# Side work of an MLP's Strassen pairs handed out at other points of the pair, and one row of means that stays in SBUF

## The chip, the cores and the metric

The kernel runs on one core of a Trainium2 chip. The metric is the device time of one execution, in microseconds (us). The kernel before takes 1814.26 us (median of 3 runs, 1813.84 to 1816.24). The five engines named below are PE (TensorE, matmul), DVE (VectorE), ACT (ScalarE), POOL (GpSimd) and SP (SyncE, which issues all DMAs here).

## The reference

The program is one layer of an encoder on 1536 tokens of width 1024: an input projection, attention and pooling heads, an output projection, then a squared-ReLU MLP and a gated per-layer embedding. The change lies in the MLP, of which the reference computes, per token,

```python
h = x + heads @ w_out
n = rmsnorm(h, g_mlp)                       # mean of squares over 1024, eps 1e-6
h = h + square(relu(n @ w_up)) @ w_down     # w_up 1024x4096, w_down 4096x1024
```

All of it is float32.

## The kernel before

**Tokens and hidden units.** The MLP works on 3 chunks `c` of 512 tokens and, in each, on 16 pairs `g` of 256 hidden units, so 48 pairs in a row, here numbered 0 to 47 (pairs 16 and 32 begin a chunk). A tile of 128x1024 floats fills one of 49 slots of SBUF, and a new tile waits until the last user of its slot is done. A float32 product is made of three fp32r matmuls, high by high, high by low, low by high (`three`), so every operand exists as a rounded high part and a low part (the rest).

**One pair.** The up projection of a pair is done by a scheme of seven half-size products instead of eight, in the order 1, 6, 2, 5, 7, 3, 4 (`Pair.run`). Each is 12 matmuls 128x256 in one of four PSUM banks: products 1 and 2 in `px`, 6 in `py`, 5 and 3 in `pz`, 7 and 4 in `pq`. Products 2, 3 and 4 add to what is in their bank, so they may start only when the bank has been read: product 3 waits for `u4` (DVE, L866), product 4 for the sum into `c2` (DVE, L870). ACT copies product 1 to `t`, DVE makes `u2`, `u4` and the four sums of `c1` and `c2`, ACT applies the ReLU and the squares, and DVE takes the low parts of the squares `r` (L886).

**The down projection** of a pair runs one pair later, in four blocks (`down`, blocks d0 to d3), each of 12 matmuls 128x512 and an evacuation on DVE that adds it to `h` (L837). They stand between the products of the next pair: product 1, d0, 6, 2, d1, 5, 7, d2, 3, 4, d3. The last product of a pair is thus followed by d3 of the pair before it, by product 1 of the next pair, and then by its own d0, which is the first to read its `r`. Inside a block the loop over the output half `e` is outside that over the hidden half `f`. With the order of `three`, the second matmul of d0 is the first that reads the low part of `r[0]`, the fifth the first that reads that of `r[1]`.

**Side work.** `after(i)` is called right behind the evacuation of each product and hands out one step each of: `feeding`, which prepares the next pair's weights (`feed`: a cast on ACT, the low part on POOL, and four sums `s1` to `s4` on DVE, L793 to L804; at its step 3 it loads the raw weights `wur` of the pair after that); `splits`, high and low parts of this pair's `w_down` (`split_down`: cast on ACT, low part on POOL for the first half, on DVE for the second, L816 and L817); in a chunk's first pair `raising` (`raise_h`, L662, multiplies `h` by the row `ws[c]` of mean squares, on DVE, eight steps); and `step()`, the next step of a list of chores: in pairs 1 to 11 or so of a chunk the squares of the next chunk (`make_m`), and the scaling, squares and gate inputs of the last one (`finishing`, with multiplications on DVE, L1138 and L1128). In the last pair of a chunk it also loads the next chunk's operands (`load_mo`). The `after` behind product 4 comes ahead of the two low parts of `r`.

**What sets the order.** PE, ACT, DVE and POOL run in the order in which the program is written, SP in an order made by a scheduler. DMAs use eight semaphores in turn, so an issue waits for the transfer eight before it.

**Mean squares of a chunk.** `make_m` ends with a row of means, brought to all partitions by a matmul, in `acc[:, 1]`; it is stored to `w_d[c]` in DRAM (L647) and loaded into `ws[c]` by `load_ms` at the chunk's first pair. `invert` later writes the reciprocals to the same `w_d[c]`. For chunk 0 this falls at the start of the MLP, where also `h` of chunk 0 comes back from DRAM (`load_h`), `h` of chunk 2 is stored there (`spill`), and `wur` of pair 1 is loaded, when `feeding` reaches its step 3.

Of the kernel before, what the change touches and what calls it, by code (L numbers as in the profile page):

```python
# [12 lines left out]
ALU = mybir.AluOpType  # L13
# [22 lines left out]
def encoder_layer(ctx, tc, xT, xn, xr, pT, w1, w2, w_pool, w_out, w_up, w_down, w_gate, w_proj,  # L36
# [23 lines left out]
    def as32(ap):  # L60
        return ap.bitcast(F32)
# [533 lines left out]
    def make_m(c, et, el):  # L595

        A, B = slice(0, HF), slice(HF, CH)
        acc = slot([P, 2, CH], F32, f"sqm{c}")  # L600

        def squares_of(b, m):
            for i in range(2):
                sq = slot([P, 2, CH], F32, f"sqm{c}{b}{i}")
                for h in range(2):
                    out = sq[:, h] if b + i + h else acc[:, 0]
                    yield ((lambda i=i, h=h, out=out: sc.activation(out, m[i][:, h], AF.Square)),
                           (lambda out=out, first=b + i + h == 0: None if first else
                            et.tensor_tensor(acc[:, 0], acc[:, 0], out, op=ALU.add)))

        for b in range(2):
            m = [slot([P, 2, CH], F32, f"m{c}_{2 * i + b}") for i in range(2)]
            for i in range(2):
                load(m[i], h_d[c][2 * i + b])
            yield from wait(5)
            yield from lagged(squares_of(b, m))
            for i in range(2):
                for h in range(2):
                    k = 2 * (2 * i + b) + h
                    sc.activation(m[i][:, h], m[i][:, h], AF.Copy, scale=gmlp_sb[:, k:k + 1])  # L620
                yield
            tt = [slot([P, 2, 2, HF], F32, f"t{c}_{b}{i}") for i in range(2)]
            t1, t2, t3, t4 = (tt[i // 2][:, i % 2] for i in range(4))
            b11, b12, b21, b22 = m[0][:, :, A], m[0][:, :, B], m[1][:, :, A], m[1][:, :, B]
            for o, x, y in ((t1, b12, b11), (t2, b22, t1), (t3, b22, b12), (t4, b21, t2)):
                et.tensor_tensor(o, x, y, op=ALU.subtract)
                yield

            def pairs():
                for i, x in ((1, b11), (6, t2), (2, b21), (5, t1), (7, t3), (3, b22), (4, t4)):  # L630
                    out = slot([P, 2, 2, HF], F32R, f"mm{c}_{i}{b}")

                    def low_part(i=i, x=x, out=out):
# [12 lines left out]
        ve.tensor_scalar(acc[:, 1], bc, 1.0 / D, EPS, op0=ALU.mult, op1=ALU.add)  # L646
        sy.dma_start(w_d[c], acc[:, 1])  # L647

    def load_mo(c, i):
        MO[c, i] = [slot([P, 4, HF], F32R, f"mo{c}_{i}{j}") for j in range(2)]  # L650
        for j in range(2):
            load(as32(MO[c, i][j]), mo_d[c][i][j])

    def load_ms(c):
        ws[c] = slot([P, CH], F32, f"w{c}")
        load(ws[c], w_d[c])
# [107 lines left out]
    class Pair:  # L764
# [62 lines left out]

        def down(self, a):
            pd = ps("d", f"pd{self.id}{a}")
            for e in range(2):  # L830
                d = 2 * a + e
                for f in range(2):
                    ws_ = [w[:, d * P:(d + 1) * P] for w in self.wd[f]]
                    for i, (w_, x_) in enumerate(three(ws_, [self.r[f][:, 0], self.r[f][:, 1]])):
                        pe.matmul(pd[:, e * CH:(e + 1) * CH], w_, x_, start=f == 0 and i == 0, stop=f == 1 and i == 2)
            h = hT[self.c][a]
            ve.tensor_tensor(h, pd.rearrange("p (a b) -> p a b", a=2), h, op=ALU.add)  # L837

        def run(self, between, after):
# [12 lines left out]
            self.product(1, x)  # L852
            sc.copy(t, x)
            after(1)
            between(0)
            y = bank("u", "py")
            self.product(6, y)
# [8 lines left out]
            ve.tensor_tensor(u4, z, u2, op=ALU.add)  # L866
            after(5)
            q = bank("u", "pq")
            self.product(7, q)
            ve.tensor_tensor(c2[:, B], q, u4, op=ALU.add)  # L870
            after(7)
            between(2)
            self.product(3, z, False)
            ve.tensor_tensor(c1[:, B], z, u2, op=ALU.add)
            sc.activation(c1[:, B], c1[:, B], AF.Relu)
            sc.activation(self.r[0][:, 0], c1, AF.Square)
            sc.activation(c1, c1, AF.Square)
# [4 lines left out]
            sc.activation(self.r[1][:, 0], c2, AF.Square)  # L882
            sc.activation(c2, c2, AF.Square)  # L883
            after(4)
            for i, x in enumerate((c1, c2)):
                ve.tensor_tensor(self.r[i][:, 1], x, as32(self.r[i][:, 0]), op=ALU.subtract)  # L886
# [12 lines left out]
    feeding = stream()  # L899
# [280 lines left out]
    for n, pair in enumerate(pairs):  # L1180
        c, g = pair.c, pair.g
        raising = None
        if g == 0:
            if c:
                for a in range(4):
                    load_h(c, a, h_d[c][a])
            load_ms(c)
            raising = raise_h(c)
        if g == 1:
            chores.append(invert(c))  # L1190
            if c:
# [12 lines left out]
        def after(i):  # L1204
            next(feeding, None)
            next(splits, None)
            if raising:
                next(raising, None)
            if g == NG - 1 and c < 2:
                load_mo(c + 1, i)  # L1210
            if n == len(pairs) - 1:
                if i == 1:
                    chores.append(first_weights())
                if i in (5, 7, 3, 4):
                    load_in(0, (5, 7, 3, 4).index(i))
            step()

        pair.run(between, after)
# [178 lines left out]
```

## Time and profile before

| | us |
|---|---|
| median of 3 runs | 1814.26 (1813.84 to 1816.24) |
| the profiled execution | 1813.31 |
| its span, first to last instruction | 1811.5 |
| PE busy | 1759.7 (97%) |
| DVE busy | 1260.0 (70%) |
| POOL busy | 1053.7 (58%) |
| ACT busy | 939.7 (52%) |
| the MLP's pairs, from product 1 of pair 0 to the last block | 579 to about 1613 |

A busy share is a mean over the span. Times within the profile are counted from the span's start. Times outside the span (1.81 us) are not broken down by the profile. In rows of an engine's timeline the first number is the start, the second the time from the first of a group's instructions to the end of the last, and a bracket gives the engine's idle time before it and what ended that; "issue" there means that the profile shows nothing that it waited for.

### The profile page before, as it was taken

Reading aid. Unit: us, or ns where it says so; the run is one execution under the profiler, and the core shown is the slowest. Engines: PE = TensorE matmul, PEld = TensorE weight load, DVE = VectorE, ACT = ScalarE, POOL = GpSimd, SP = SyncE. Lnnn points to the kernel's source line nnn. Section 1 sums busy time; section 2 is a strip of 40 time slices with the busy share of each in tenths; the row PEclk is TensorE's granted clock in tenths of the full one; section 3 lists DMA queues with packets and bytes.
Section 4 is the critical chain, followed back from the end, with each engine's and each line's share of the span. In section 5 each row is a group of like instructions: output and inputs, shape, how many; then the busy total and the mean of one; then the engine's idle time right before and its main releaser. Section 6 shows DMA issues by size and latency. Waiting matters only on the chain.

```text
span 1811.5 us, 28604 instructions
## 1 busy us (share of the span) xinstructions
PE 1759.7 (97%) x10540; PEld 1537.1 (85%) x10540; DVE 1260.0 (70%) x1843; ACT 939.7 (52%) x1854; POOL 1053.7 (58%) x923
## 2 busy tenths in 40 slices
PE   9999899999999799999999999999999999999997
PEld 7888777888868798988888889889898999888887
DVE  5677865888894677865568877876776556665655
ACT  6434455768794455655445545554455444443332
POOL 3474774535674567676656776785577666543121
PEclk9999999999999899999999999999999999999998
DMA  6333545120519335343364442556443323272102
GB/s 248 114 123 105 216 165 185 36 94 13 206 46 367 139 122 198 121 177 100 136 265 157 163 151 96 195 185 235 179 157 100 110 94 99 89 262 70 59 12 82
DMA packets 83883, 256.84 MB, mean 142 GB/s; under 512 B 9888, under 2 KB 16416, under 8 KB 83744
## 3 DMA queue, kind: packets, MB, share of 16 engines
q1 hardware_dynamic: 83744, 255.02, 39.7%
q8 instruction: 83, 1.36, 0.3%
q14 instruction: 56, 0.46, 0.1%
HBM read 195.74 MB, written 59.24 MB: 141 GB/s over the span
## 4 chain that ended last, share of the span: by engine, by line
PE 78%; DVE 7%; ACT 5%; DMA 3%; issue 3%; POOL 1%; POOLq 0%; DVEq 0%; ACTq 0%; SPq 0%
PE pd L49 25%; PE z L49 7%; PE px L49 6%; PE pz L49 6%; PE pq L49 6%; PE pg L49 6%; PE py L49 4%; PE pp L49 3%; PE o L49 3%; PE tp L53 3%; PE po L49 3%; PE S L49 3%; PE pj L49 1%; DMA wur<-in_w_up_dram 1%; DVE r L886 1%
## 5 line engine op out<-in xcount | busy, mean ns | idle before, releaser
L49 PE MATMUL pd<-r,wd 128*128 128x512 f32 x2304 | 568.5, 395 | 10.8 <-DVE r L886 10.6
L49 PEld LDWEIGHTS pd<-r,wd 128*128 128x128 f32 x2304 | 419.5, 188 | 100.3 <-DVE r L886 16.1
L787 POOL TENSOR_TENSOR w<-ws,w 128x512 fp32r<-128x512 f32 x192 | 272.5, 1423 | 217.9 <-ACT w L786 206.8
L787 POOL TENSOR_TENSOR w<-wur,w 128x512 fp32r<-128x512 f32 x144 | 212.8, 1489 | 135.4 <-ACT w L786 134.4
L837 DVE TENSOR_TENSOR h<-pd,h 128x1024 f32<-128x1024 f32 x192 | 233.5, 1216 | 76.6 <-PE pd L49 76.5
L786 ACT CAST w<-ws 128x512 fp32r<-128x512 f32 x192 | 118.5, 617 | 271.1 <-DVE ws L795 241.1
L461 POOL TENSOR_SCALAR pr<-pr,rr 128x512 f32<-128x512 f32 x160 | 111.2, 705 | 134.7 <-DVE rr L456 66.8
L49 PE MATMUL z<-w,x 128*128 128x512 f32 (+1 forms) x864 | 175.7, 359 | 0.9 <-DVE w L160 0.5
L49 PEld LDWEIGHTS pz<-mo,w 128*128 128x128 f32 x1152 | 150.7, 190 | 19.3 <-issue 11.2
L49 PEld LDWEIGHTS z<-w,x 128*128 128x128 f32 x864 | 142.9, 189 | 28.0 <-ACT w L159 2.1
L49 PE MATMUL pz<-mo,w 128*128 128x256 f32 x1152 | 153.6, 283 | 10.2 <-issue 10.2
L817 DVE TENSOR_TENSOR wd<-wdr,wd 128x512 fp32r<-128x512 f32 x96 | 102.8, 1071 | 83.1 <-ACT wd L816 76.6
L49 PE MATMUL pq<-mo,w 128*128 128x256 f32 x1152 | 153.7, 283 | 1.0 <-issue 1.0
L49 PE MATMUL px<-mo,w 128*128 128x256 f32 x1152 | 152.2, 281 | 0.0
L49 PEld LDWEIGHTS px<-mo,w 128*128 128x128 f32 x1152 | 146.5, 189 | 4.0
L49 PEld LDWEIGHTS pq<-mo,w 128*128 128x128 f32 x1152 | 144.7, 191 | 1.4 <-issue 1.3
L49 PE MATMUL pg<-hg,wg 128*128 128x512 f32 (+1 forms) x768 | 141.0, 338 | 0.2
L472 ACT CAST pt<-tp 128x512 fp32r<-128x512 f32 x160 | 88.0, 591 | 88.5 <-PE tp L53 86.8
L49 PEld LDWEIGHTS pg<-hg,wg 128*128 128x128 f32 x768 | 118.6, 188 | 17.8 <-DVE hg L1128 1.0
L817 POOL TENSOR_TENSOR wd<-wdr,wd 128x512 fp32r<-128x512 f32 x96 | 131.8, 1373 | 2.6 <-DMA w_d<-sqm 2.6
L886 DVE TENSOR_TENSOR r<-c,r 128x512 fp32r<-128x512 f32 x96 | 74.7, 783 | 74.1 <-ACT c L883 46.2
L473 DVE TENSOR_TENSOR pt<-tp,pt 128x512 fp32r<-128x512 f32 x160 | 104.0, 684 | 31.4 <-ACT pt L472 31.1
(195 smaller groups left out, 3036.2 us busy)
## 6 DMA issues: line engine op xcount, KB each, us to landing
wur<-in_w_up_dram SPq DMA_DIRECT2D x96, 512.0 KB, 4.2
wdr<-in_w_down_dram SPq DMA_DIRECT2D x96, 512.0 KB, 4.4
mo_d<-mm SPq DMA_DIRECT2D x84, 256.0 KB, 2.3
mo<-mo_d SPq DMA_DIRECT2D x42, 512.0 KB, 7.7
h_d<-h SPq DMA_DIRECT2D x16, 512.0 KB, 3.0
h<-h_d SPq DMA_DIRECT2D x16, 512.0 KB, 9.9
xn<-in_xn_dram SPq DMA_DIRECT2D x12, 512.0 KB, 6.4
qs_d<-qs SPq DMA_DIRECT2D x12, 512.0 KB, 3.0
```

What stands on the lines that cost most here:

```text
L49: last_pe[0] = nc.tensor.matmul(*a, **k).ins
L53: last_pe[0] = nc.tensor.transpose(*a, **k).ins
L461: gp.tensor_scalar(p, p, rr, 1.0, op0=ALU.mult, op1=ALU.mult)
L472: sc.copy(self.pt[kt][:, 0], tp)
L473: ve.tensor_tensor(self.pt[kt][:, 1], tp, as32(self.pt[kt][:, 0]), op=ALU.subtract)
L786: sc.copy(t[:, 0], x)
L787: gp.tensor_tensor(t[:, 1], x, as32(t[:, 0]), op=ALU.subtract)
L817: (gp, ve)[i].tensor_tensor(lo, self.dr[i][:, h], as32(hi), op=ALU.subtract)
L837: ve.tensor_tensor(h, pd.rearrange("p (a b) -> p a b", a=2), h, op=ALU.add)
L886: ve.tensor_tensor(self.r[i][:, 1], x, as32(self.r[i][:, 0]), op=ALU.subtract)
```

## The change

Five edits.

1. `after` becomes two functions. `used(i)` holds the loads of the last pairs and is called directly behind product i's matmuls. `hook()` hands out the side work, seven times a pair as before, but behind: product 1's copy, product 6's sum, product 2's ReLU, block d1, product 5's sum, the low parts of `r`, and block d3. None stands behind products 7, 3 and 4.
2. The low parts of `r` come directly behind the squares, ahead of the sixth hook.
3. In `down`, `f` is the outer loop, so the low part of `r[1]` is first read by the eighth matmul of a block instead of the fifth.
4. Chunk 0's row of mean squares is used where it is, in SBUF: no store, no load.
5. `wur` of pair 1 is loaded ahead of chunk 0's `h`, not in `feeding`.

```diff
-        sy.dma_start(w_d[c], acc[:, 1])
+        if c:
+            sy.dma_start(w_d[c], acc[:, 1])
+        else:
+            ws[0] = acc[:, 1]
...
-            for e in range(2):
-                d = 2 * a + e
-                for f in range(2):
+            for f in range(2):
+                for e in range(2):
+                    d = 2 * a + e
...
+            def product(i, out, fresh=True):
+                self.product(i, out, fresh)
+                used(i)
+
+            def square(i, x):
+                sc.activation(self.r[i][:, 0], x, AF.Square)
+                sc.activation(x, x, AF.Square)
+
+            def low_part(i, x):
+                ve.tensor_tensor(self.r[i][:, 1], x, as32(self.r[i][:, 0]), op=ALU.subtract)
...
-            after(1)
+            hook()
             between(0)
...
             ve.tensor_tensor(u2, y, t, op=ALU.add)
-            after(6)
-            self.product(2, x, False)
+            hook()
+            product(2, x, False)
             sc.activation(c1[:, A], x, AF.Relu)
-            after(2)
+            hook()
             between(1)
+            hook()
             z = bank("tp", "pz")
-            self.product(5, z)
+            product(5, z)
             ve.tensor_tensor(u4, z, u2, op=ALU.add)
-            after(5)
+            hook()
...
             ve.tensor_tensor(c2[:, B], q, u4, op=ALU.add)
-            after(7)
             between(2)
...
-            after(3)
-            self.product(4, q, False)
+            square(0, c1)
+            product(4, q, False)
...
-            after(4)
-            for i, x in enumerate((c1, c2)):
-                ve.tensor_tensor(self.r[i][:, 1], x, as32(self.r[i][:, 0]), op=ALU.subtract)
+            square(1, c2)
+            low_part(0, c1)
+            low_part(1, c2)
+            hook()
             between(3)
+            hook()
...
-                if i == 3 and n + 1 < len(pairs):
+                if i == 3 and 0 < n < len(pairs) - 1:
                     pairs[n + 1].load_up()
...
     load_mo(0, ORDER[5]), load_mo(0, ORDER[6])
+    pairs[1].load_up()
     for a in range(4):
         load_h(0, a, h_d[0][a])
...
-            load_ms(c)
+                load_ms(c)
...
-        def after(i):
+        def hook():
             next(feeding, None)
             next(splits, None)
             if raising:
                 next(raising, None)
+            step()
+
+        def used(i):
             if g == NG - 1 and c < 2:
                 load_mo(c + 1, i)
...
-            step()
```

SP at the start of the MLP, before: `mo0_41` is the last operand of pair 0's product 4, `h00` to `h03` are chunk 0's `h`, `h_d2_*` the stores of chunk 2's `h`, `w_d0` and `w0` the row of means, `wur0_1*` pair 1's raw weights; a bracket lists the semaphores that the issue waits for.

```order
L56 DMA h00_6357<-h_d0_0_304 128x1024 [waits DMAHW0_49,PE_49]
L56 DMA h01_6359<-h_d0_1_305 128x1024 [waits DMAHW1_49]
L56 DMA h02_6361<-h_d0_2_306 128x1024 [waits DMAHW2_49,PE_49]
L56 DMA h03_6363<-h_d0_3_307 128x1024 [waits DMAHW3_49]
L647 DMA w_d0_259<-sqm0_4189 128x512 [waits DMAHW4_49,DVE_49]
L708 DMA h_d2_0_312<-h20_5526 128x1024 [waits DMAHW5_49,DVE_49]
L708 DMA h_d2_1_313<-h21_5528 128x1024 [waits DMAHW6_49,DVE_49]
L708 DMA h_d2_2_314<-h22_5530 128x1024 [waits DMAHW7_49,DVE_49]
L56 DMA wur0_10_6531<-in_w_up_dram 128x1024 [waits DMAHW0_49,PE_49]
L56 DMA wur0_11_6532<-in_w_up_dram 128x1024 [waits DMAHW1_49,Activation_49]
L56 DMA w0_6556<-w_d0_259 128x512 [waits DMAHW4_49,DMAHW2_49,Pool_49]
```

The same engine and place in the changed kernel:

```order
L56 DMA wur0_10_6357<-in_w_up_dram 128x1024 [waits DMAHW0_49,PE_49]
L56 DMA wur0_11_6358<-in_w_up_dram 128x1024 [waits DMAHW1_49]
L56 DMA h00_6361<-h_d0_0_304 128x1024 [waits DMAHW2_49,PE_49]
L56 DMA h01_6363<-h_d0_1_305 128x1024 [waits DMAHW3_49]
L56 DMA h02_6365<-h_d0_2_306 128x1024 [waits DMAHW4_49,PE_49]
L56 DMA h03_6367<-h_d0_3_307 128x1024 [waits DMAHW5_49]
L711 DMA h_d2_0_312<-h20_5526 128x1024 [waits DMAHW6_49,DVE_49]
L711 DMA h_d2_1_313<-h21_5528 128x1024 [waits DMAHW7_49,DVE_49]
```

Pair 1's weights moved from behind the first stores of `h_d2` to ahead of `h00`; the store and the load of the row are gone, and `h_d2_0` now signals on semaphore 6 instead of 5.

ACT in pair 0, before: the ReLU of product 2 (`c0_0<-px0_0`) and the casts behind it; `wd0_010` is the high part of the second half of pair 0's `w_down`.

```order
L861 ACTIVATE c0_0_6559<-px0_0_6562 128x256 [waits PE_49]
L786 CAST w0_0_4_6620<-wur0_01_6098 128x512 [waits DMAHW1_49]
L816 CAST wd0_010_6582<-wdr0_01_6346 128x512 [waits DMAHW3_49]
L786 CAST w0_1_1_6646<-wur0_10_6531 128x512 [waits DMAHW0_49,Pool_49]
L816 CAST wd0_010_6582<-wdr0_01_6346 128x512
```

The same rows in the changed kernel:

```order
L876 ACTIVATE c0_0_6556<-px0_0_6559 128x256 [waits PE_49]
L789 CAST w0_0_4_6617<-wur0_01_6098 128x512 [waits DMAHW1_49]
L819 CAST wd0_010_6579<-wdr0_01_6346 128x512 [waits DMAHW6_49,DMAHW3_49]
L789 CAST w0_1_1_6629<-wur0_10_6357 128x512 [waits DMAHW0_49]
L819 CAST wd0_010_6579<-wdr0_01_6346 128x512
```

The order is the same, but the slot of `wd0_010` is another one, and its first cast now also waits for semaphore 6, that of the store of `h_d2_0`.

DVE in pair 20 (chunk 1, `g` 4; names with `1_4`), from block d1's evacuation on, before: `u1_4<-pz` is `u4`, `ws1_50` the sums `s1` and `s2` for pair 21, `wd1_411` a low part of `w_down`, `h03` a chore of `finishing`, `r1_40` and `r1_41` the low parts of the squares.

```order
L837 TENSOR_TENSOR h11_10035<-pd1_31_11021,h11_10035 128x1024
L866 TENSOR_TENSOR u1_4_10937<-pz1_4_11039,u1_4_10937 128x256
L793 TENSOR_TENSOR ws1_50_11053<-wur1_51_10917 128x512
L817 TENSOR_TENSOR wd1_411_10962<-wdr1_41_10811,wd1_410_10961 128x512
L1138 TENSOR_TENSOR h03_6363<-h03_6363,w0_10261 128x512
L870 TENSOR_TENSOR c1_4_10938<-pq1_4_11062,u1_4_10937 128x256
L795 TENSOR_TENSOR ws1_50_11053<-ws1_50_11053,wur1_50_10916 128x512
L837 TENSOR_TENSOR h12_10037<-pd1_32_11087,h12_10037 128x1024
L874 TENSOR_TENSOR c1_4_10938<-pz1_4_11039,u1_4_10937 128x256
L880 TENSOR_TENSOR c1_4_10938<-pq1_4_11062,u1_4_10937 128x256
L801 TENSOR_TENSOR ws1_51_11054<-wur1_50_10916,wur1_51_10917 128x512
L886 TENSOR_TENSOR r1_40_10939<-c1_4_10938,r1_40_10939 128x512
```

The same place in the changed kernel:

```order
L840 TENSOR_TENSOR h11_10032<-pd1_31_11018,h11_10032 128x1024
L796 TENSOR_TENSOR ws1_50_11036<-wur1_51_10930 128x512
L820 TENSOR_TENSOR wd1_411_10959<-wdr1_41_10808,wd1_410_10958 128x512
L1152 TENSOR_TENSOR h03_6367<-h03_6367,w0_10258 128x512
L882 TENSOR_TENSOR u1_4_10934<-pz1_4_11045,u1_4_10934 128x256
L798 TENSOR_TENSOR ws1_50_11036<-ws1_50_11036,wur1_50_10929 128x512
L886 TENSOR_TENSOR c1_4_10935<-pq1_4_11070,u1_4_10934 128x256
L840 TENSOR_TENSOR h12_10034<-pd1_32_11084,h12_10034 128x1024
L889 TENSOR_TENSOR c1_4_10935<-pz1_4_11045,u1_4_10934 128x256
L893 TENSOR_TENSOR c1_4_10935<-pq1_4_11070,u1_4_10934 128x256
L864 TENSOR_TENSOR r1_40_10936<-c1_4_10935,r1_40_10936 128x512
L864 TENSOR_TENSOR r1_41_10937<-c1_4_10935,r1_41_10937 128x512
```

Three pieces of side work moved from behind `u4` to ahead of it, and none is left between the last sums and the low parts. On ACT the cast of the next pair's weights that stood between the two pairs of squares now follows both.

More of the change, by code (lines that the diff above doesn't have):

```diff
@@ L837, in down, with run @@
             ve.tensor_tensor(h, pd.rearrange("p (a b) -> p a b", a=2), h, op=ALU.add)
-        def run(self, between, after):
+        def run(self, between, used, hook):
             A, B = slice(0, HF), slice(HF, CH)
@@ L849, in bank @@
                 return (tp_ps(f"{nm}{self.id}") if tag == "tp" else ps(tag, f"{nm}{self.id}"))[:, 0:HF]
+            def product(i, out, fresh=True):
[6 more added lines that the diff above has]
+                ve.tensor_tensor(self.r[i][:, 1], x, as32(self.r[i][:, 0]), op=ALU.subtract)
             x = bank("tp", "px")
-            self.product(1, x)
+            product(1, x)
@@ L853, in run @@
             sc.copy(t, x)
-            after(1)
+            hook()
             between(0)
             y = bank("u", "py")
-            self.product(6, y)
+            product(6, y)
             ve.tensor_tensor(u2, y, t, op=ALU.add)
-            after(6)
-            self.product(2, x, False)
+            hook()
+            product(2, x, False)
             sc.activation(c1[:, A], x, AF.Relu)
-            after(2)
+            hook()
             between(1)
+            hook()
             z = bank("tp", "pz")
-            self.product(5, z)
+            product(5, z)
@@ L866, in run @@
             ve.tensor_tensor(u4, z, u2, op=ALU.add)
-            after(5)
+            hook()
             q = bank("u", "pq")
-            self.product(7, q)
+            product(7, q)
             ve.tensor_tensor(c2[:, B], q, u4, op=ALU.add)
-            after(7)
             between(2)
-            self.product(3, z, False)
+            product(3, z, False)
             ve.tensor_tensor(c1[:, B], z, u2, op=ALU.add)
             sc.activation(c1[:, B], c1[:, B], AF.Relu)
-            sc.activation(self.r[0][:, 0], c1, AF.Square)
@@ L1215, in after @@
                     load_in(0, (5, 7, 3, 4).index(i))
-            step()
-        pair.run(between, after)
+        pair.run(between, used, hook)
         for _ in splits:
```

3 lines of the change are left out of this document (removed).

## The prediction

> **What bounds the kernel now.** I read the page first, then the table of stages, PE's waits in the MLP, and the timelines where those waits lie.
>
> ```profile
> span 1811.5 us, 28604 instructions
> PE 1759.7 (97%) x10540; PEld 1537.1 (85%) x10540; DVE 1260.0 (70%) x1843; ACT 939.7 (52%) x1854; POOL 1053.7 (58%) x923
> ```
>
> The profiled execution took 1813.31 us, so 1.81 us lie outside its span, and it is 0.95 us below the median of 1814.26. PE is busy for all but 51.8 us of the span. The change removes no matmul, so it can win only where PE waits or runs at a lowered clock. Two stages, the first 29 us of the MLP and the rest up to its end (busy time of PE first, then PEclk, DMA share and GB/s at the end of a row):
>
> ```profile
> 579.00:608.00 29.00, 17.30 (x111) 15.98 (x110) 17.11 (x24) 11.52 (x22) 14.73 (x12) 0.82 0.73 283
> 608.00:1613.00 1005.00, 995.02 (x6208) 891.46 (x6207) 696.73 (x886) 519.07 (x970) 660.74 (x470) 1.00 0.44 152
> ```
>
> The start is idle for 11.7 us and at 0.82 of the clock; the other 1005 us are idle for 10.0 us only. What PE waits for in the two, by the view of its waits:
>
> ```profile
> PE pd L49 <- DVE r L886: 10.6, 11, 1.8
> PE pz L49 <- issue: 10.2, 3, 9.2
> PE pq L49 <- issue: 1.0, 2, 0.5
> ```
>
> So nearly all is at two points: block d0 waiting for the low part of `r`, and products 3 and 4 (`pz`, `pq`) waiting for `u4` and `c2`. The latter is 9.2 us once, at the start, and about 0.5 us twice at the other chunks' starts. PE's timeline at the start:
>
> ```profile
> 583.28 1.59 PE L49 MATMUL pz<-mo,w 128*128 128x256 f32 x12
> 584.71 1.57 PE L49 MATMUL pq<-mo,w 128*128 128x256 f32 x12
> 595.48 2.90 PE L49 MATMUL pz<-mo,w 128*128 128x256 f32 x12 [9.20 <-issue]
> 598.18 2.76 PE L49 MATMUL pq<-mo,w 128*128 128x256 f32 x12
> 600.74 1.61 PE L49 MATMUL px<-mo,w 128*128 128x256 f32 x12
> 602.18 0.40 PE L49 MATMUL pd<-r,wd 128*128 128x512 f32 x1
> 604.34 0.96 PE L49 MATMUL pd<-r,wd 128*128 128x512 f32 x3 [1.77 <-DVE r L886]
> 606.04 2.12 PE L49 MATMUL pd<-r,wd 128*128 128x512 f32 x8 [0.74 <-DVE r L886]
> 607.99 1.60 PE L49 MATMUL py<-mo,w 128*128 128x256 f32 x12
> ```
>
> By its starts a product takes 1.43 us (583.28 to 584.71). Product 3 could start at 586.14 and starts at 595.48: 9.34 us lost. Products 3 and 4 then take 2.70 and 2.56 instead of 1.43 each, 2.4 us lost to the clock, and d0 takes 5.81 (602.18 to 607.99) where a free block takes 2.79 (below), 3.0 us lost. That is 14.7 us at the start.
>
> ```profile
> 595.50:599.00 3.50, 3.50 (x16) 3.50 (x17) 3.50 (x8) 0.62 (x1) 0.16 (x1) 0.50 0.25 98
> ```
>
> The granted clock right after the gap is 0.50, which is what doubles those two products.
>
> **The start: chunk 0's row and pair 1's weights.** DVE ahead of `u4` (L866), and, from the chain of waits, the load of `h00`:
>
> ```profile
> 592.22 0.69 DVE L662 TENSOR_TENSOR h<-h,w 128x512 f32<-128x512 f32 x1 [11.38 <-DMA w<-w_d]
> ...
> 594.36 0.68 DVE L662 TENSOR_TENSOR h<-h,w 128x512 f32<-128x512 f32 x1
> 594.96 0.42 DVE L866 TENSOR_TENSOR u<-pz,u 128x256 f32<-128x256 f32 x1
> ```
>
> ```profile
> 569.53 11.30 DMA h<-h_d
> ```
>
> DVE stands 11.38 us behind the load of the row `w`. It has left, but DVE's next wait is near: `h00` and a cast. `h00` landed at 580.83 and now has two transfers of 512 KB more ahead of it. The stage is full of transfers:
>
> ```profile
> 560.00:579.00 19.00, 19.00 (x159) 18.73 (x157) 8.55 (x18) 4.26 (x8) 5.58 (x5) 1.00 1.03 411
> h_d<-h SPq DMA_DIRECT2D x1, 512.0 KB, 9.6
> ```
>
> At 411 GB/s 512 KB (524,288 bytes) take 1.28 us, so `h00` lands at about 580.83 + 2.56 = 583.4. Were it this alone, `u4` would stand behind four multiplications, two `wd` and `s1`, seven pieces of 0.60 us (594.36 to 594.96), and behind `u2` with 0.3: 583.4 + 4.2 + 0.3 + 0.42, product 3 at about 588.4. But ACT's cast `wd0_010` now waits for the store of `h_d2_0` (semaphore 6, in the order above). That store (the second row above, the DMA issued at 577.05) landed 9.6 us later, at 586.65; with two transfers of 1.28 put ahead and the row's 256 KB (0.64) gone, 588.6. The cast adds 0.6, so `wd` on DVE starts at 589.2. Up to `u4` come that `wd`, a multiplication, `s1`, a second `wd` and a second multiplication, five spacings of 0.60, so `u4` starts at 592.2, takes 0.42, and product 3 follows at 592.6. A piece may wait for a POOL operation (`s1` below takes 1.56 once, 0.9 above its 0.68), and the second `wd` needs a second cast behind the first: upper bound 594.0. I take 593.7. The idle time is still above 7 us, so I keep the half clock: 593.7 + 2.70 + 2.56 + 1.44 (product 1) = 600.4 for d0, 2.79 more with 0.6 left of the wait for `r`, 603.8 for `py` against 607.99. **Gain 4.2**, bounds 1.5 (the store lands 2.7 later, as other transfers are issued sooner) and 7 (592.6, the clock back after one product, no wait of d0).
>
> The Trainium skill ("TensorE: Matmul & The Clock Gate", What's actually happening) has the clock set by how busy PE was in a free-running window of about 3.4 us. The trace agrees: 9.2 us idle, 0.50 behind it. By that rule the 7 us left here still cost the half clock, and a gap under one window would not.
>
> **d0's wait for `r`: edits 1, 2 and 3.** 10.6 us idle over 11 blocks, of which 2.5 (1.77 + 0.74) are pair 1's, counted above; 8.1 are left in ten pairs. The largest is d0 in pair 21. DVE and PE, and one row of ACT, there:
>
> ```profile
> 1024.16 0.41 DVE L866 TENSOR_TENSOR u<-pz,u 128x256 f32<-128x256 f32 x1
> 1024.49 1.56 DVE L793 TENSOR_TENSOR ws<-wur 128x512 f32<-128x512 f32 x1
> ...
> 1035.12 1.32 DVE L886 TENSOR_TENSOR r<-c,r 128x512 fp32r<-128x512 f32 x1 [1.61 <-ACT c L883]
> ```
>
> ```profile
> 1023.84 2.95 PE L49 MATMUL pd<-r,wd 128*128 128x512 f32 x12
> 1026.63 1.60 PE L49 MATMUL pz<-mo,w 128*128 128x256 f32 x12
> ...
> 1033.71 1.27 PE L49 MATMUL pd<-r,wd 128*128 128x512 f32 x4
> 1036.50 2.15 PE L49 MATMUL pd<-r,wd 128*128 128x512 f32 x8 [1.52 <-DVE r L886]
> 1038.49 0.75 PE L49 MATMUL py<-mo,w 128*128 128x256 f32 x5
> ```
>
> ```profile
> 1032.63 0.60 ACT L786 CAST w<-wur 128x512 fp32r<-128x512 f32 x1
> ```
>
> A free block takes 2.79 (1023.84 to 1026.63), this one 4.78 (1033.71 to 1038.49): 1.99 lost for 1.52 idle, 1.31 per us. Ten pairs lose about 8.1 x 1.31 = 10.6. Taken away from the wait: the cast that stands between the squares (1032.63, its place 0.51 by ACT's next start), and three matmuls of 2.79 / 12 = 0.23, 0.70 us, by which the low part is read later. So it is asked for at 1033.71 + 7 x 0.23 = 1035.3 and ready at 1035.12 - 0.51 + 0.69 (the length without a POOL operation) = 1035.3 to 1035.9. What took 1.52 is then 0 to 0.6 in the worst pair and nothing in those that waited 0.3 to 0.9 us. **Gain 10.0** of 10.6; bounds 6.5 (0.4 left in each of ten) and 10.6.
>
> **Chunk starts (pairs 16 and 32).**
>
> ```profile
> 1280.34 1.14 DVE L662 TENSOR_TENSOR h<-h,w 128x512 f32<-128x512 f32 x1 [7.16 <-DMA w<-w_d]
> 1286.31 1.64 PE L49 MATMUL pz<-mo,w 128*128 128x256 f32 x12 [0.52 <-issue]
> ```
>
> `w` is late behind a burst of loads, and DVE, once held, is still behind when `u4` is due. Product 3 idles 0.52 here and product 4 0.5 by PE's waits, and as much at the other start: 2.0 us, which at the 1.31 of above cost 2.6. The row of these chunks still goes through DRAM. But `used` issues the first two loads of the next chunk's operands behind the matmuls of product 1 of the pair before, not behind an evacuation and its side work, so I expect them out of the burst: 2 x 1.28 = 2.6 us, `w` at 1277.7. Then DVE is free when block d1 is evacuated, and `u4` is on time. **Gain 2.5**; bounds 2.6 and, since hook 4 now puts three pieces of 0.60 ahead of `u4` and if `w` lands no earlier, a loss of 1.8 in each chunk, -3.6.
>
> **The new wait: hook 4 ahead of `u4`.** DVE's `u4` and PE's product 3 in a plain pair, and what `s1` takes in all 48 (least, median, most ns):
>
> ```profile
> 1518.41 0.42 DVE L866 TENSOR_TENSOR u<-pz,u 128x256 f32<-128x256 f32 x1 [0.21 <-PE pz L49]
> 1522.41 1.57 PE L49 MATMUL pz<-mo,w 128*128 128x256 f32 x12
> ```
>
> ```profile
> L793 DVE TENSOR_TENSOR ws<-wur x48: 673/681/1809, 571.1 to 1582.0; 128x512 f32<-128x512 f32 x48
> ```
>
> `u4` ends at 1518.83, 3.58 us ahead of product 3. Hook 4 queues `s1` and `wd` ahead of it, 1.2 to 1.4 us: hidden by products 7 and d2 with over 2 us left. In busy pairs it isn't: in pair 20, where DVE comes to `u4` only at 1024.16, the three pieces (`s1` with 1.56, two of 0.60) put its end at 1024.16 + 2.8 + 0.4 = 1027.4 against product 3 at 1026.63, 0.8 late. By the same sum from their own rows two more are late, pair 19 by 0.9 and pair 35 by 0.3; the rest of the busy ones come out on time within 0.1. 2.0 us late in all; as the wait also lets `r`'s chain off, I price it at 1.5, bounds 0 and 9 (ten busy pairs at 0.9). What else hides: product 4's `c2` stands behind hook 5 as it stood behind `after(5)`; the hooks behind d3 put casts ahead of the next `t`, which isn't read until product 6's sum, a block later.
>
> The row that speaks against this is `s1` with up to 1809 ns: the length goes up when POOL is at work on SBUF. The Trainium skill ("SBUF — State Buffer", SBUF: two separate sides) calls it an exclusive lock between a DVE operation with two SBUF inputs and a POOL operation that reads SBUF; the 1.56 in pair 20 beside 0.68 alone agrees.
>
> **The sum.** 4.2 + 10.0 + 2.5 - 1.5 = 15.2 less: 1813.3 - 15.2 = 1798.1, and by the 0.95 to the median 1799.0.
>
> **The rivals.**
>
> *The start's gap closes (0.15).* If the store of `h_d2_0` lands before the cast needs it, `u4` ends near 588 and product 3 starts at 588.4. For it: the DMA that DVE is seen to wait for is the row's load alone, and the stores can be issued as soon as output projections end. Against: the stage is full, and the store can't overtake the six loads. It would save 7.1 there; the gap from 586.14 is then 2.3, and after the 1.52 idle of pair 21's d0 eight matmuls take 1.99 (1036.50 to 1038.49), 0.25 each, so the clock may stay full and save 2.4 more, and d0's 3.0 shrinks by 2.7: 12.2 in place of 4.2, so 1791.
>
> *Hook 4 gives back what d0 wins (0.12).* The ten pairs that waited for `r` are those with much on DVE; `u4` queued behind three pieces may be late in all of them: 9 lost in place of 1.5, and `w` no earlier at chunk starts. 1799 + 7.5 = 1806.5. For: pairs 19 and 20. Against: the median of `s1`, 681 ns, says that in most pairs no POOL operation is met.
>
> *Slower: each piece of hook 4 meets a POOL operation (0.05).* Three pieces at the most that `s1` has taken, 1.81, are 5.4: `u4` would end 1.8 later than product 3 wants it in the plain pair above (3.58). Against gains of 16.7 (4.2, 10.0 and 2.5) it decides from 16.7 / 1.8, about 9 pairs; only pairs with a multiplication or a chore on DVE have three pieces, and in 20 of these 36 would be lost: 1814.3 - 16.7 + 36 = 1833.6. For: POOL is 58% busy. Against: the same median.
>
> *It doesn't do what it says (0.06).* d0 still waits, because the chain on ACT from product 4's sum to the last square is what is long, and the new cast keeps the gap at the start: both gains under 3 us in sum, 1812 to 1815. Against: the cast at 1032.63 and the 1.32 of the low part, which are side work by the rows above.
>
> **How the numbers follow.** The forecast, 0.62, is 1799, its own range 1794 to 1804 (start 1.5 to 7, d0 6.5 to 10.6, not all at their ends at once). 1791 and 1806.5 lie on either side; a range from 1789 to 1807 holds the three, less their tails, and leaves out the two last cases. 0.2%, 3.6 us, is what a measurement can tell from no change: faster 0.89, the same 0.06, slower 0.05.
>
> **What would show it.** Right: DVE has no wait for `w` in pair 0; ACT's first cast of `wd0_010` waits for a DMA until about 588.6; product 3 of pair 0 starts 1 to 3 us earlier with a clock of 0.50 behind it; PE's waits on `r` fall from 10.6 to 1 or 2 us; small waits of `pz` appear in pairs 19, 20 and 35; the idle time at chunk starts is gone. Wrong: product 3 of pair 0 at about 588 (the first rival); `pz` waiting in ten pairs or more (the second and third); `pd` still waiting 8 us (the last).

## The result: slower by 1.5%

The changed kernel takes 1842.71 us (median of 5 runs, 1842.06 to 1843.24) against 1815.36 for the kernel before in its runs. The ratio is 1.0151, 95% interval 1.0136 to 1.0166: 27 us slower, where 15 us faster was forecast.

The page of the profile after, its first lines, and PE's waits in the MLP:

```profile
span 1840.9 us, 28622 instructions
PE 1771.5 (96%) x10540; PEld 1546.9 (84%) x10540; DVE 1319.1 (72%) x1843; ACT 945.2 (51%) x1854; POOL 1072.6 (58%) x923
```

```profile
PE pz L49 <- DVE u L882: 25.9, 16, 3.4
PE pz L49 <- issue: 10.7, 3, 7.5
...
PE pd L49 <- DVE r L864: 0.2, 1, 0.2
```

Three things stand out. The wait of d0 for `r` is gone (10.6 us before, 0.2 now), as forecast. In its place product 3 (`pz`) waits for `u4` in 16 pairs, 25.9 us. And DVE is busy for 1319.1 us instead of 1260.0 with the same 1843 instructions: 59 us more for the same work.

The books, by the starts of the pairs in the two traces: pair 1 starts 2.0 us sooner (600.74 to 598.76); pairs 1 to 46 take 1021.5 us instead of 990.5, 31.0 more; pair 47 and the rest take 0.4 more. That is the 29.4 us between the spans. Inside the 31.0 the d0 blocks give back 13.7 us, pair 1's among them, so the rest of the pairs loses 44.7, nearly all of it ahead of or in products 3 and 4. That is more than the 25.9 us of waits, and part of the difference is the clock: behind the four long waits of pairs 5, 19, 25 and 28 (2.4 to 3.4 us) the granted clock stood at 0.50, for 17 us in all, and products 3 and 4 of these four pairs take 7.1 us longer than in a plain pair. Before, the clock was 1.00 from 608 to 1613.

Pair 20 again, DVE from the low parts of pair 19 to `u4`, then PE and POOL:

```profile
1023.93 0.69 DVE L864 TENSOR_TENSOR r<-c,r 128x512 fp32r<-128x512 f32 x1 [1.38 <-ACT c L861]
1024.54 1.22 DVE L840 TENSOR_TENSOR h<-pd,h 128x1024 f32<-128x1024 f32 x1
1025.68 0.68 DVE L804 TENSOR_TENSOR ws<-wur,wur 128x512 f32<-128x512 f32 x1
1026.28 1.79 DVE L807 TENSOR_TENSOR ws<-wur,ws 128x512 f32<-128x512 f32 x1
1027.99 1.78 DVE L1142 SCALAR_TENSOR_TENSOR hg<-h,gple_sb,hg 128x512 fp32r<-128x512 f32 x1
...
1036.06 1.21 DVE L840 TENSOR_TENSOR h<-pd,h 128x1024 f32<-128x1024 f32 x1
1037.19 0.68 DVE L796 TENSOR_TENSOR ws<-wur 128x512 f32<-128x512 f32 x1
1037.79 1.78 DVE L820 TENSOR_TENSOR wd<-wdr,wd 128x512 fp32r<-128x512 f32 x1
1039.49 1.75 DVE L1152 TENSOR_TENSOR h<-h,w 128x512 f32<-128x512 f32 x1
1041.16 0.41 DVE L882 TENSOR_TENSOR u<-pz,u 128x256 f32<-128x256 f32 x1
```

```profile
1036.73 2.95 PE L49 MATMUL pd<-r,wd 128*128 128x512 f32 x12
1041.72 1.68 PE L49 MATMUL pz<-mo,w 128*128 128x256 f32 x12 [2.04 <-DVE u L882]
```

```profile
1024.49 1.30 POOL L790 TENSOR_TENSOR w<-wur,w 128x512 fp32r<-128x512 f32 x1 [5.12 <-ACT w L789]
1025.75 1.77 POOL L1161 TENSOR_TENSOR sqg<-sqg,sqg 128x512 f32<-128x512 f32 x1
1027.48 1.75 POOL L790 TENSOR_TENSOR w<-ws,w 128x512 fp32r<-128x512 f32 x1
```

From 1024.54 to `u4` DVE has hardly a gap: it is one full queue of 16.6 us, and seven of its pieces, the rows left out among them, take 1.56 to 1.79 us, where `ws` and `h` pieces alone take 0.68. POOL had been idle for 5.12 us up to 1024.49, and from there it works without a pause too. Where two such pieces meet, the engines take turns: DVE's pieces that end at 1028.07 and 1029.77 do so 0.55 and 0.54 us behind the ends of POOL's at 1027.52 and 1029.23. How general the lengthening is shows in the length of two sums, `s4` and `s1` (least, median, most in ns), after and before:

```profile
L807 DVE TENSOR_TENSOR ws<-wur,ws x48: 676/1786/1797, 580.6 to 1622.7; 128x512 f32<-128x512 f32 x48
...
L796 DVE TENSOR_TENSOR ws<-wur x48: 673/1404/1791, 571.6 to 1610.3; 128x512 f32<-128x512 f32 x48
```

```profile
L804 DVE TENSOR_TENSOR ws<-wur,ws x48: 672/680/1789, 580.1 to 1593.7; 128x512 f32<-128x512 f32 x48
```

`s4` went from a median of 680 to 1786 ns, `s1` from 681 to 1404.

### The profile page after: what moved, and what is told of

It is laid out like the page before. It is cut to its first block, busy times and chain, and to the rows that moved or that the text cites. A ratio compares the mean times of both kernels' runs of the same rounds, so it can differ in the third digit from the quotient of the medians.

```text
span 1840.9 us, 28622 instructions
## 1 busy us (share of the span) xinstructions
PE 1771.5 (96%) x10540; PEld 1546.9 (84%) x10540; DVE 1319.1 (72%) x1843; ACT 945.2 (51%) x1854; POOL 1072.6 (58%) x923
## 4 chain that ended last, share of the span: by engine, by line
PE 40%; DVE 6%; issue 5%; POOL 4%; ACT 3%; DMA 1%; POOLq 0%; DVEq 0%; SPq 0%; ACTq 0%
PE pd L49 17%; PE pg L49 6%; PE pq L49 4%; PE px L49 4%; PE pz L49 4%; PE py L49 2%; POOL w L790 2%; PE pj L49 1%; POOL wd L820 1%; DVE wd L820 1%; DVE h L840 1%; DVE h L1152 1%; ACT w L789 0%; DVE hg L1142 0%; ACT r L860 0%
## 5 line engine op out<-in xcount | busy, mean ns | idle before, releaser
L790 POOL TENSOR_TENSOR w<-ws,w 128x512 fp32r<-128x512 f32 x192 | 289.2, 1511 | 149.9 <-ACT w L789 137.6
L49 PE MATMUL pz<-mo,w 128*128 128x256 f32 x1152 | 157.8, 287 | 36.6 <-DVE u L882 25.9
L820 DVE TENSOR_TENSOR wd<-wdr,wd 128x512 fp32r<-128x512 f32 x96 | 109.7, 1142 | 83.7 <-ACT wd L819 78.0
L49 PE MATMUL pq<-mo,w 128*128 128x256 f32 x1152 | 158.4, 288 | 2.1 <-DVE c L886 1.7
L49 PEld LDWEIGHTS pq<-mo,w 128*128 128x128 f32 x1152 | 148.4, 195 | 3.7 <-issue 2.7
L820 POOL TENSOR_TENSOR wd<-wdr,wd 128x512 fp32r<-128x512 f32 x96 | 137.6, 1433 | 0.0
L864 DVE TENSOR_TENSOR r<-c,r 128x512 fp32r<-128x512 f32 x96 | 66.5, 692 | 88.1 <-ACT c L861 84.7
```

Source lines behind the costliest of these rows:

```text
L49: last_pe[0] = nc.tensor.matmul(*a, **k).ins
L790: gp.tensor_tensor(t[:, 1], x, as32(t[:, 0]), op=ALU.subtract)
L820: (gp, ve)[i].tensor_tensor(lo, self.dr[i][:, h], as32(hi), op=ALU.subtract)
```

## The experiments

Times are medians; the kernel before, run beside each group, had medians of 1815.28 (e1 to e4), 1814.35 (e5 to e8), 1814.48 (e9 to e12) and 1813.94 us (e13). "Hooks" are the seven places of side work, in their order.

**Which hooks cost.** First question: is it the fourth hook, now ahead of `u4`, or the sixth and seventh, now behind product 4 and d3?

Hooks 4 and 5 back (e1):

```diff
             between(1)
-            hook()
             z = bank("tp", "pz")
...
             ve.tensor_tensor(c2[:, B], q, u4, op=ALU.add)
+            hook()
             between(2)
```

> The changed kernel with two of the seven places put back: no side work behind block d1, and one hook behind product 7's sum again; the hooks behind the low parts and behind d3 stay. In the profile of the changed kernel product 3 (or the block ahead of it) loses about 43 us in pairs 2 to 46. Theory A, the fourth hook alone costs that, because its three DVE pieces now stand ahead of u4: nearly all comes back, product 3 has no wait outside the chunk starts, 1800 to 1804 us. Theory B, the sixth and seventh hooks cost it, because they now stand behind product 4 and d3 and push their work into the first half of the next pair, so that d1's evacuation ends up to 3 us late: u4 is in time but product 4's c2 then comes late in its place, 1825 to 1835 us. Both halves: 1810 to 1820 us.

Measured: 1832.71 us, ratio 1.0100 (1.0085 to 1.0115). `u4` is in time, but product 4 waits 18.6 us for `c2` in its place. Ten us came back, not 43: theory A falls.

Only hooks 4 and 5 moved (e2): the changed kernel with the other four edits undone and hooks 6 and 7 behind the squares; the last pairs' loads stay directly behind the matmuls.

> The kernel before with only the fourth and fifth side work steps moved (behind d1 and behind u4), and the last pairs' loads behind the matmuls; e outside f in the blocks, the row through DRAM, pair 1's weights in the stream, the other hooks as before. Theory A (the fourth hook ahead of u4 is the cost by itself): 1840 to 1850 us, with product 3 waiting for u4 in some 16 pairs. Theory B (it needs the later hooks too): by the pairs' spare time in the profile of before only pairs 19, 20 and 35 and the two chunk starts are late, together about 6 us: 1817 to 1822 us.

Measured: 1814.93 us, ratio 0.9997 (0.9987 to 1.0006), no change that can be told. That is a balance: PE waits 2.6 us for `u4`, four times, and 4.3 us more at the three chunk starts (14.5 against 10.2, the rows of `pz` with "issue"), while d0's wait falls from 10.6 to 5.6 us. Away from the chunk starts the fourth hook alone costs little more than the prediction said.

Hooks 6 and 7 back (e3):

```diff
             square(0, c1)
+            hook()
             product(4, q, False)
...
             square(1, c2)
+            hook()
             low_part(0, c1)
             low_part(1, c2)
-            hook()
             between(3)
-            hook()
```

> The changed kernel with the sixth and seventh hooks put back behind product 3's and product 4's squares, ahead of the low parts; the fourth stays ahead of u4. Theory A: still 1835 to 1842 us. Theory B: product 3's waits fall to the 6 us of pairs 19, 20, 35 and the chunk starts, and d0 keeps most of its gain through the order of f and e: 1805 to 1811 us.

Measured: 1806.65 us, ratio 0.9956 (0.9941 to 0.9970). Moving these two hooks, and nothing else, is worth 36 us. Its waits:

```profile
PE pz L49 <- issue: 8.1, 3, 7.0
PE pz L49 <- DVE u L882: 4.3, 4, 1.6
PE pd L49 <- DVE r L864: 1.8, 1, 1.8
```

All hooks back, the other edits kept (e4): the two diffs above together.

> The changed kernel with all seven hooks where after(i) stood; kept are the loads behind the matmuls, f outside e, the row in SBUF and pair 1's early weights. By both theories faster than before: the start's 2.6 us and two thirds of d0's 10 us: 1805 to 1809 us. It says what the other edits are worth alone.

Measured: 1803.19 us, ratio 0.9936 (0.9921 to 0.9950), better than forecast for it. It beats both kernels.

**What in the late hooks costs.** Four kernels keep hook 4 ahead of `u4`.

Hook 6 behind product 3's squares, hook 7 directly behind the low parts (e5):

```diff
             square(0, c1)
+            hook()
             product(4, q, False)
...
             low_part(1, c2)
             hook()
             between(3)
-            hook()
```

> The changed kernel (fourth hook ahead of u4) with the sixth hook behind product 3's squares again, and the seventh directly behind the low parts of r, not behind d3; so the gap from the seventh hook to the next pair's first is block d3 and product 1 as before, and no side work stands ahead of the low parts in the last hook. The kernel with both put back took 1806.65 us. Theory B1 (it is the crowding of five hooks between d3 and d1 that costs, as engines run their side work in order and find too little time for it): 1803 to 1808 us. Theory B2 (any side work that comes later than the low parts costs): 1815 to 1825 us.

Measured: 1830.26 us, ratio 1.0087 (1.0072 to 1.0102), 24 us more than e3. Neither reading was right; this is the most telling pair of the study. Between e3 and e5 ACT, POOL and SP have the same instructions in the same order, and on DVE only the pieces of one hook stand behind the two low parts instead of ahead of them. Pair 20's start on DVE in e3, then in e5, from the last sum of `c2` on:

```profile
1002.64 0.42 DVE L894 TENSOR_TENSOR c<-pq,u 128x256 f32<-128x256 f32 x1 [0.90 <-PE pq L49]
1002.99 0.68 DVE L804 TENSOR_TENSOR ws<-wur,wur 128x512 f32<-128x512 f32 x1
1004.46 0.69 DVE L864 TENSOR_TENSOR r<-c,r 128x512 fp32r<-128x512 f32 x1 [0.79 <-ACT c L861]
1006.83 1.29 DVE L864 TENSOR_TENSOR r<-c,r 128x512 fp32r<-128x512 f32 x1 [1.68 <-ACT c L861]
```

```profile
1012.04 0.42 DVE L894 TENSOR_TENSOR c<-pq,u 128x256 f32<-128x256 f32 x1 [0.85 <-PE pq L49]
1013.97 0.69 DVE L864 TENSOR_TENSOR r<-c,r 128x512 fp32r<-128x512 f32 x1 [1.50 <-ACT c L861]
1016.33 1.28 DVE L864 TENSOR_TENSOR r<-c,r 128x512 fp32r<-128x512 f32 x1 [1.67 <-ACT c L861]
1017.54 1.77 DVE L804 TENSOR_TENSOR ws<-wur,wur 128x512 f32<-128x512 f32 x1
```

In e3 the sum `s3` runs in DVE's wait for ACT's squares and takes 0.68. In e5 that wait is idle, and `s3` comes when POOL is at work: 1.77. DVE's busy time in the whole of e5 is 1337.2 us against 1261.9 in e3.

Hook 6 behind product 3's squares, hook 7 behind d3 (e6): as e5, with the second `hook()` behind `between(3)`.

> As the last, but the seventh hook behind d3, one product ahead of the next pair's first hook, the sixth behind product 3's squares. B1: four hooks are still crowded, so about half of the 36 us between the changed kernel (1842.7) and the one with both back (1806.65): 1820 to 1830 us. B2: as the run before it or little more. If only the sixth hook's place mattered: 1807 us.

Measured: 1820.89 us, ratio 1.0037 (1.0024 to 1.0050), the size forecast for crowding, but later should have been worse than e5 and is better by 9 us. Here `s3` comes behind d3's evacuation and DVE's busy time is only 1266.0: some of the loss is not in the total length.

Only chores late (e7), and only weight parts late (e8): `hook` got two flags, so that at each of the four places one half is handed out.

```diff
-        def hook():
-            next(feeding, None)
-            next(splits, None)
-            if raising:
-                next(raising, None)
-            step()
+        def hook(parts=True, chore=True):
+            if parts:
+                next(feeding, None)
+                next(splits, None)
+                if raising:
+                    next(raising, None)
+            if chore:
+                step()
```

> The changed kernel with the two late hooks split: the next pair's weight parts come behind product 3's and product 4's squares as before, only the chores (squares and operands of the next chunk, scaling of the last) come behind the low parts and behind d3. If the backlog is of the total side work on DVE and POOL, both halves cost: 1815 to 1830 us. If the weight parts being late is what counts (each step of theirs feeds the next one through ACT, POOL and DVE): 1806 to 1810 us. If the chores are: 1835 to 1843 us.

> The other half: chores behind the squares as before, the weight parts behind the low parts and behind d3. Total backlog: 1815 to 1830 us; weight parts: 1835 to 1843 us; chores: 1806 to 1810 us.

Measured: e7 1825.62 us, ratio 1.0062 (1.0047 to 1.0077); e8 1828.08, ratio 1.0073 (1.0056 to 1.0089). Both halves cost, 19 and 21 us over e3, so it is the sum of side work. DVE is busy for 1264.0 us in e7 and 1320.6 in e8: the lengthening in total comes with the weight parts, and e7 loses its 19 us without it.

**Is it the meeting with POOL?** The low parts of the up weights, POOL's largest work, are left out, and POOL writes zeros there, which reads no SBUF. In the changed kernel (e9) and in e3's order (e10):

```diff
-                gp.tensor_tensor(t[:, 1], x, as32(t[:, 0]), op=ALU.subtract)
+                gp.memset(as32(t[:, 1]), 0.0)
```

> The changed kernel, but the low parts of the up weights aren't computed: POOL writes zeros there instead (an operation that reads no SBUF). To be compared with the same edit made to the kernel with hooks six and seven back; the two kernels without it stand 36 us apart (1842.7 and 1806.65). Theory L, the loss is DVE pieces made longer because in their late places they meet POOL operations that read SBUF (DVE's busy time rose by 59 us): the pair of kernels without such operations comes out within 10 us of each other. Theory Q, it is DVE's queue itself, pieces no longer done while DVE waits for the squares: they stay 25 us or more apart.

> The kernel with hooks six and seven back, with the same zeros in place of the low parts of the up weights. It is the base for the run before it: near 1800 us, 4 to 8 below the 1806.65 of the same order with the low parts, as its few u4 waits go. Theory L: the run before it is within 10 us of this one. Theory Q: 25 us or more above.

Measured: e9 1794.39 us, ratio 0.9890 (0.9875 to 0.9905); e10 1796.18, ratio 0.9901 (0.9886 to 0.9915). The 36 us between the two orders are gone; the changed order is no slower now. Of e9 the page and `s4`:

```profile
span 1793.0 us, 28554 instructions
...
PE 1755.2 (98%) x10540; PEld 1538.1 (86%) x10540; DVE 1182.4 (66%) x1843; ACT 940.9 (52%) x1854; POOL 723.6 (40%) x923
```

```profile
L807 DVE TENSOR_TENSOR ws<-wur,ws x48: 677/684/689, 581.9 to 1576.0; 128x512 f32<-128x512 f32 x48
```

But POOL also has 349 us less to do here, as a write of zeros takes 0.53 us. So the last run (e13) writes them three times:

```diff
-                gp.memset(as32(t[:, 1]), 0.0)
+                for _ in range(3):
+                    gp.memset(as32(t[:, 1]), 0.0)
```

> The changed kernel's order of side work, with POOL writing zeros three times in place of each low part of the up weights (three times 0.53 us by the run with one), so that POOL is as long at work as with the low parts but reads no SBUF for it; the low parts aren't computed. If what the run with one write took away is the meeting of DVE pieces with POOL operations that read SBUF: 1793 to 1800 us, DVE's pieces at 0.68. If it was POOL being relieved (its queue holding slots and weights back): half or more of the loss comes back, 1818 us or more.

Measured: 1796.09 us, ratio 0.9906 (0.9889 to 0.9922).

```profile
PE 1757.8 (98%) x10540; PEld 1540.7 (86%) x10540; DVE 1188.5 (66%) x1843; ACT 941.4 (52%) x1854; POOL 1078.8 (60%) x1595
```

POOL is busy for 1078.8 us, as long as in the changed kernel, and nothing is lost. So it is not POOL's load. And where DVE's pieces run beside the writes of zeros, they keep their short length; a `wd` and a multiplication of `h`, DVE first, then POOL:

```profile
1009.79 0.69 DVE L821 TENSOR_TENSOR wd<-wdr,wd 128x512 fp32r<-128x512 f32 x1 [1.76 <-ACT wd L820]
1010.40 0.68 DVE L1153 TENSOR_TENSOR h<-h,w 128x512 f32<-128x512 f32 x1
```

```profile
1009.13 3.33 POOL L791 MEMSET w<- 128x512 f32 x6
```

In pair 20 of the changed kernel such pieces took 1.78 and 1.75 beside POOL's low parts. From 600 to 1600 us of e13, 86 of the sums `ws` ran beside writes of zeros alone, and each took 0.67 to 0.68 us. So what lengthens the pieces is that POOL's operations read SBUF while DVE's pieces do.

**The other edits.** Stores ahead of loads at the start (e11), on e4: `pairs[1].load_up()` and `load_h(0, 2)`, `load_h(0, 3)` moved from ahead of the `while fill` loop to behind it, so that the first two stores of `h_d2` are issued ahead of them.

> The kernel with all hooks back (1803.19 us), and at the start of the MLP the first two stores of chunk 2's h issued ahead of pair 1's weights and of the second half of chunk 0's h. The cast of w_down then has no store to wait for. If that store is what holds product 3 of pair 0 now (the cast began 0.1 us behind the store's landing): product 3 starts at about 586 instead of 592.6, product 4 at 589 to 590 behind the weights of pair 1, and the clock comes back sooner: 1794 to 1798 us. If it is the flood of transfers as a whole: 1801 to 1804.

Measured: 1803.24 us, ratio 0.9938 (0.9921 to 0.9954), the same as e4. Product 3 of pair 0 does start sooner, 589.78 against 592.56, but product 4 then waits 1.40, up to 0.10 behind the end of `c2`'s sum on DVE (593.24 + 0.41), and the clock is lowered all the same (below).

```profile
589.78 2.57 PE L49 MATMUL pz<-mo,w 128*128 128x256 f32 x12 [2.28 <-issue]
593.75 2.90 PE L49 MATMUL pq<-mo,w 128*128 128x256 f32 x12 [1.40 <-issue]
```

`e` outside `f` again (e12), on e4: edit 3 undone alone.

> The kernel with all hooks back, with e outside f in the down blocks again (edit 3 undone alone). d0 waits 5.0 us there; the low part of r[1] is asked for 0.70 us sooner in each of the seven or eight blocks that are near: 4 to 7 us slower than 1803.19, so 1807 to 1810 us. If the order of the matmuls doesn't matter: 1803.

Measured: 1810.70 us, ratio 0.9978 (0.9969 to 0.9987): the order of the matmuls is worth 7.5 us, a little more than expected; d0's waits are 10.3 us in it against 5.0 in e4.

## Why the prediction was wrong

**The start: right.** Product 3 of pair 0 starts at 594.22 (forecast 593.7), held by the store of `h_d2_0` through the cast of `wd0_010`, as worked out (forecast 588.6 for its landing):

```profile
588.95 0.62 ACT L819 CAST wd<-wdr 128x512 fp32r<-128x512 f32 x1 [4.10 <-DMA h_d<-h]
```

The clock behind it was 0.50, and pair 1 starts 2.0 us sooner with 2.6 less lost in its d0: 4.6 against 4.2 forecast. That the sum is so close is in part luck: product 3 came 0.5 us later than forecast, and product 4 took 1.84 instead of 2.56, as the clock came back during it.

**d0: right, in place and size.** 10.6 us of waits fell to 0.2. Edit 3 carries about half of that (10.3 us in e12, 5.0 in e4); the rest came with the places of the hooks.

**Chunk starts: the gain didn't come.** `w` did land sooner against its pair's start, by 1.6 us in pair 16 and 1.2 in pair 32 (2.6 forecast), but the blocks ahead of product 3 lose 1.7 and 1.8 us there, more than before, as hook 4's three pieces stand ahead of `u4`. With hooks 6 and 7 back (e3) they lose 0.5 and 1.0, with all back (e4) 0.2 each.

**The step that failed: "the rest of the busy ones come out on time within 0.1", the price of 1.5 us for hook 4.** That sum took the spare time of `u4` in each pair, and the lengths of the pieces, from rows of before. Both rest on where hooks 6 and 7 stand. The prediction weighed moving them for ACT (a cast out of the squares) and for the low parts, and for what stands ahead of `t`; their pieces on DVE were costed at nothing and not followed. With those hooks in place the price stays inside its bounds of 0 and 9, if above 1.5: product 3 waits for `u4` 2.6 us in e2 and 4.3 in e3, and e3 takes 3.5 us more than e4. With them late, the blocks ahead of product 3 and products 3 and 4 lose some 42 us in pairs 1 to 46. Three things come together, by the rows of pair 20, by e3 against e5 and by e9, e10 and e13. DVE waits for ACT's squares with nothing to do, where `s3` or a chore used to run. Hooks 6, 7, 1, 2 and 3 then fall between product 4 and block d1, and POOL, which in pair 20 had been idle for 5.12 us, works without a pause through the same stretch. So DVE's pieces meet POOL's and take up to 1.8 us instead of 0.68, DVE's queue is full to `u4`, and product 3 waits.

The slower rival named the lengthening, but for hook 4's three pieces only, at 1.8 us with product 3 late by about 1.8 us, and got 1833.6 for 20 pairs; in pair 20 seven pieces are long, and five of them stand ahead of hook 4. What was held against it was the median of `s1`, 681 ns. That was a fact of the old order: in the new one it is 1404. A length that depends on what another engine does at that moment can't be carried over to an order in which that moment moves. The chance of 0.05 was far too small for that reason.

The Trainium skill ("SBUF — State Buffer", SBUF: two separate sides) says that a DVE operation with two SBUF inputs and a GpSimd operation that reads SBUF exclude each other for the whole instruction. The runs agree: in pair 20 the two take turns, and beside writes of zeros in place of POOL's low parts `s4` is back at a median of 684 ns and the kernel at 1794 (e9) and 1796 us (e13).

**What stays open.** e6 loses 14 us against e3 with DVE busy for only 4 us more, and e7 loses 19 with 2 more. Some of that must be pieces that come late without being longer in total, or lengthening moved into the pairs that have no room; the runs don't divide it. A write of zeros also waits for no cast, whereas the changed kernel's POOL stood idle for 326 us for ACT's casts ahead of these low parts; what that freedom is worth in e9 and e13 was not measured apart. The kernel before was not run with zeros in place of the low parts, so what the meetings cost it is unknown; e3's order gained 10.5 us by it.

## What to carry to other kernels

Side work in an engine's wait for another is free only there: when it is moved, ask what that wait is then filled with, and which engine runs beside the new place. Where two engines shut each other out of SBUF, a piece's length is a property of the schedule and not of the piece; price it at both lengths, 0.68 and 1.78 us here, for every piece whose neighbours move, and count the pieces up to the point where the next one is needed (`u4`). Total busy time with an unchanged instruction count (1260 to 1319 us) is the quickest sign of it, but its absence proves nothing: e6 and e7 lost 14 and 19 us with 4 and 2 us more.

## What the runs showed of the hardware

The TensorE clock fell behind a shorter idle time than expected. In e11 PE was idle for 2.28 us ahead of product 3 and 1.40 ahead of product 4 (rows above); the granted clock in the stretches behind them (PE, PEld, DVE, ACT and POOL busy, then PEclk):

```profile
589.80:593.70 3.90, 2.55 (x12) 2.25 (x12) 3.90 (x5) 0.00 (x0) 2.37 (x2) 0.55 1.03 419
593.75:597.00 3.25, 3.25 (x15) 3.25 (x16) 3.25 (x5) 2.33 (x5) 1.28 (x1) 0.50 0.82 330
```

In pair 20 of the changed kernel 2.04 us idle left the clock at 1.00, in the stretch that begins with its product 3:

```profile
1041.70:1045.00 3.30, 3.28 (x26) 3.26 (x27) 2.41 (x5) 2.74 (x5) 1.31 (x1) 1.00 0.41 166
```

So the first rival's hope, that a gap of 2.3 us keeps the clock, failed in the one run that made such a gap. The prediction's rule from the Trainium skill ("TensorE: Matmul & The Clock Gate", What's actually happening), by which a gap under one window of about 3.4 us costs nothing, does not hold here as it was put.

In these traces the place of a gap on a fixed grid decides, and not its length alone. In each of the fifteen traces the changes of the granted clock in the MLP lie on a grid of 3.41 us, and a stretch of full clock was followed by one at 1.00 when PE was idle in it for up to 1.89 us, and by one at 0.50 when PE was idle for 1.90 us or more (30 times). Of the gap of 2.04 us in pair 20, 1.89 us lay in one stretch (PE busy for 1.52 of 3.41); the wait in pair 28 and the gap in e11 lay wholly in one. The rows are the stretch with pair 20's gap, the one with pair 28's and the one behind that, all of the changed kernel, and then the one with e11's gap:

```profile
1038.16:1041.57 3.41, 1.52 (x7) 0.91 (x5) 3.41 (x4) 0.00 (x0) 2.54 (x2) 1.00 0.02 6
1222.48:1225.89 3.41, 1.01 (x8) 0.76 (x7) 3.41 (x4) 0.13 (x1) 3.34 (x2) 1.00 0.70 167
1225.90:1229.30 3.40, 3.40 (x18) 3.40 (x18) 2.26 (x4) 2.19 (x4) 2.15 (x2) 0.50 0.96 354
```

```profile
586.77:590.18 3.41, 1.13 (x10) 0.95 (x9) 3.41 (x4) 1.14 (x2) 3.41 (x3) 1.00 1.03 412
```
